# Casting w_out's lower left quarter ahead of the frames' last parts, and issuing the gate's rows behind the first roots

## The chip, the core and the metric

The kernel runs on one core of a Trainium2 chip. The time is the device time of one execution in microseconds (us); lower is better. The engines that matter are TensorE (PE, matrix products), VectorE (DVE), ScalarE (ACT), GpSimd (POOL), and SyncE (SP), which here only issues DMAs. Each engine takes its instructions strictly in the order in which the built program lists them.

## What is computed

One layer of a streaming encoder for 2048 prompt frames and 32 sample frames of width 1024:

```python
hn = rmsnorm(h, g_mix)
proj = hn @ w_in                                   # 1024 x 3072
...                                                # conv mixer and pooling mixer give yA, yB
h = h + jnp.concatenate([yA, yB], axis=-1) @ w_out     # 1024 x 1024
gate = jax.nn.sigmoid(rmsnorm(h, g_ple) @ w_ple_gate)  # 1024 x 1024
h = h + (p @ w_ple) * gate
return rmsnorm(h, g_final)
```

Everything is float32. The kernel reaches that precision on PE by splitting a number into a rounded part (the *cast*, made on ACT) and the *rest* (the number minus its cast, made on DVE), and by forming three products of such parts for each product.

## The kernel before

The program has three stages: the input projection with the mixers (to about 537 us), the w_out stage (to about 706 us), and the embedding products and the gate stage. The change is in the first two pairs of the w_out stage.

**A pair.** The w_out stage takes the mixers' output y from memory (`y_d`, transposed) and goes over the frames in pairs of 128. A pair is multiplied by the 1024 x 1024 weight with seven half-sized products instead of eight (`seven`), each 12 matmuls of 128 x 512. Weights and frames are cut into quarters for it: the weight's quarters 11, 21 (lower left) and 22 (lower right) and the combinations T1 to T4; the frame parts 11, 12, 22 and the combinations S1 to S4. Three banks of PSUM hold the sums and give the tiles their names: `x_o`, `y_o`, `z_o`. The order on PE within a pair is 11·11 (x_o), the first half of S1·T1 (z_o), S2·T2 (x_o), the second half of S1·T1, S3·T3 (x_o), 12·21 (y_o), S4·22 (z_o), and 22·T4 (x_o). Between two products that share a bank, DVE or ACT reads the bank out (`carry` and `out` in `h_ops`, lines 1335 and 1340). So 22·T4 may not start before DVE has added S3·T3 to the tile x.

**Frame parts.** `frame_parts` makes them: a combination is one DVE instruction (`comb`, line 201, tiles `y_fS`), then `split` (lines 80 and 83) makes the cast on ACT and the rest on DVE (tiles `y`, `y_S`). It makes S1, 11, S2 and S3 at once and hands back `more`, which makes 12, S4 and 22. The parts of the next pair are made while PE works on this one; their buffers (pool `cmb`, eight) come free as the products of the pair before end.

**Weight quarters.** The combinations T1 to T4 are made during the last group of the projection. The quarters 11, 21 and 22 are made at the start of the w_out stage by `layout` (casts at line 1408, rests at line 1409; tiles `wo_c` and `wo_d`), from raw rows `wo_q`, which `load_bottom` (line 334) loads. In the first pair, `seven` calls `rest` after its first product: it makes all of 12, S4 and 22 and then, through `tc.issue_after`, the quarters 21 and 22, row block by row block.

**The gate's rows.** The gate's weight has to be scaled row by row with g_ple before the gate stage. That is done on the side in the w_out stage: `scale_gate(k)` loads two halves of a row block (`gs`, line 1387, issued by POOL), and its `rest` scales them on ACT (line 1391) and stores them to `g_d` from ACT's DMA queue (line 1392). `next_gate` first scales what was loaded at the call before, then issues the next loads; it is called at the end of every pair and once inside the second. The two buffers of `gs` are used again and again, so a load waits for the store of the row before. The scaling keeps its place in the program's order on ACT.

**After a pair**, `done_h` squares the finished rows on ACT (line 93), makes the root of the norm on POOL (`rstd_of`, lines 72 and 76) and stores the rows to `h_d` from SP (line 1361).

**What sets the order.** The code calls the steps in one order, and a scheduler arranges them for each engine by estimated costs, within the dependences. `tc.issue_after(ins)` keeps what is called under it behind `ins`, and `tc.keep_in_program_order` keeps an instruction at its place. A tile pool hands a buffer on, and the new user waits for the old ones; `reuse_waits="tile"` sets how finely.

Of the kernel before, what the change touches and what calls it, by code (L numbers as in the profile page):

```python
# [10 lines left out]
F32R = mybir.dt.float32r  # L11
AF = mybir.ActivationFunctionType
ALU = mybir.AluOpType
PSUM = bass.MemoryType.PSUM

P = 128
# [11 lines left out]
NH = D // 2  # L28
KH = KC // 2
# [5 lines left out]
def trunk(ctx, tc, x_p, x_s, c_conv, c_pool, p_p, p_s, g_mix, w_in, conv_w, conv_b, pool_w,  # L35
          pool_scale, w_out, g_ple, w_gate, w_ple, g_fin, y_p, y_s, sc_p, sp_p, sc_s, sp_s):
    nc = tc.nc
# [28 lines left out]
    nhalf = const.tile([P, 1], F32, name="nhalf")  # L66
    nc.gpsimd.memset(nhalf, -0.5)

    def rstd_of(ssq, n, name, r=None):

        ms = sm.tile([P, 1], F32, tag="ms", name=f"ms_{name}")
        nc.gpsimd.tensor_scalar(ms[:n], ssq[:n], scalar1=1.0 / D, scalar2=EPS,  # L72
                                op0=ALU.mult, op1=ALU.add)
        if r is None:
            r = sm.tile([P, 1], F32, tag="rstd", name=f"rstd_{name}")
        nc.gpsimd.tensor_tensor(r[:n], ms[:n], nhalf[:n], op=ALU.pow)  # L76
        return r

    def split(hi, lo, src, eng=nc.vector, later=False):
# [108 lines left out]
    def frame_parts(cmb, tmp, name, a11, a12, a21, a22):  # L188

        A = {}

        def put(q, src):
            A[q] = cmb.tile([P, KH, 2, P], F32R, tag="c", name=f"{name}_{q}")
            return split(A[q][:, :, 0], A[q][:, :, 1], src)

        def comb(q, x, y, op):
            t = tmp.tile([P, KH, P], F32, tag="s", name=f"{name}_f{q}")  # L200
            nc.vector.tensor_tensor(t, x, y, op=op)
            return t

        s1 = comb("S1", a21, a22, ALU.add)
        put("11", a11)
        s2 = comb("S2", s1, a11, ALU.subtract)
        put("S2", s2)
        put("S1", s1)
        put("S3", comb("S3", a11, a21, ALU.subtract))

        def more():
            put("12", a12)
            put("S4", comb("S4", a12, s2, ALU.subtract))
            return put("22", a22)

        return A, more

    def seven(name, A, W, carry, out, between={}, late=False, in_parts=False, first_tile=False, end=None):

        step = lambda c: between[c]() if c in between else None
        frames_late, weights_late = (FINE, FINE[::2] + FINE[1:2]) if in_parts else (None, None)
        X, Y, Z = (bank(f"{c}_{name}") for c in "xyz")

        def lower(*parts):
            for ks in parts:
                product(Z, A["S1"], W["T1"], P, ks.start == 0, ks)
            return carry(Z, (1, 1)) if ks.stop == KH else None

        parts = range(KH // 2), range(KH // 2, KH)
        product(X, A["11"], W["11"], P, True, order=frames_late)
        c1 = carry(X, (0, 0))
        step(1)

        def upper():
            product(Y, A["12"], W["21"], P, True, order=weights_late)
            out(Y, c1, (0, 0))

        if not late:
            upper()
        if late:
            lower(parts[0])
        step(2)
        product(X, A["S2"], W["T2"], P, False)  # L250
        c2 = carry(X, (0, 1))
        step(3)
        c3 = lower(parts[1]) if late else lower(range(KH))
        step(4)

        def right():
            product(Z, A["S4"], W["22"], P, False, order=weights_late)
            out(Z, c2, (0, 1))

        if first_tile:  # L260
            right()
        product(X, A["S3"], W["T3"], P, False)
        out(X, c3, (1, 1))
        step(5)
        if late:
            upper()
        if not first_tile:
            right()
        step(6)
        if end is not None:  # L270
            end(X)
            return
        product(X, A["22"], W["T4"], P, False)
        out(X, None, (1, 0))
# [67 lines left out]
    with ExitStack() as s1:  # L342
        pool = lambda name, bufs: s1.enter_context(tc.tile_pool(name=name, bufs=bufs))
# [16 lines left out]
        def put(piece, src, later=False):  # L360

            split(piece[:, :, 0], piece[:, :, 1], src, later=later)
# [405 lines left out]
        rows = ftile("rows").rearrange("p k n -> p (k n)")[:112, :P]  # L768
# [502 lines left out]
        for gi, tbs in enumerate(GROUPS):  # L1271
            if gi == 2:

                frames_in.close()
                t = slot("hn_4")
# [3 lines left out]
                W = sums_slots("wo")  # L1279
# [35 lines left out]

    with ExitStack() as s2:
        pool = lambda name, bufs: s2.enter_context(tc.tile_pool(name=name, bufs=bufs, reuse_waits="tile"))
        w3, qa, xh, st, ss, cmb = (pool(*a) for a in (
            ("w3", 1), ("qa", 2), ("xh", 3), ("st", 4), ("ss", 3), ("cmb", 8)))

        def quarters(name, W):
            c = halves(slot(f"{name}_c"))
            d = {h: w3.tile([P, KH, NH], F32R, tag=f"d{h}", name=f"{name}_d{h}") for h in (1, 0, 2)}
            W.update({"11": c[:2], "21": (c[2], d[0]), "22": (d[1], d[2])})

        def whole_quarters(W, k, top, bot):
# [6 lines left out]
        def h_ops(x, n, name, bare=False, two=False):  # L1333

            add = lambda o, a, b: nc.vector.tensor_tensor(o, a, b, op=ALU.add)  # L1335

            def carry(ps, at):
                t = st.tile([P, NH], F32, tag="t", name=f"c_{name}_{at[0]}{at[1]}")
                if bare and at != (1, 0):
                    nc.scalar.copy(t[:n], ps[:n])  # L1340
                    return t
                add(t[:n], ps[:n], half_of(x, at, n))
                if two:
                    add(t[:n], ps[n:2 * n], t[:n])
                return t

            def out(ps, c, at):
                t = half_of(x, at, n)
                if bare and at != (1, 0):
                    add(t, t, c[:n])  # L1350
                    c = None
                add(t, ps[:n], t if c is None else c[:n])
                if two:
                    add(t, ps[n:2 * n], t)

            return carry, out
# [22 lines left out]
        def scale_gate(k):  # L1379

            ts = [qa.tile([P, NH], F32, tag="q", name=f"gs_{k}_{half}") for half in range(2)]
            rows = w_gate.rearrange("(q k c) n -> k q c n", q=4, k=KC)[k]
            for half, t in enumerate(ts):
                nc.gpsimd.dma_start(t, rows[:, :, half * NH:half * NH + NH])

            def rest():
                for half, t in enumerate(ts):  # L1390
                    tc.keep_in_program_order(nc.scalar.activation(t, t, AF.Copy, scale=vec[:, 100 + k:101 + k]))
                    nc.scalar.dma_start(g_d[k * P:k * P + P, half * NH:half * NH + NH], t)

            return rest
# [8 lines left out]
        def layout(parts):  # L1403
            for k in range(KH):
                for q, t, c in ("11", tops[k // 2], k % 2), ("21", bots[k], 0), ("22", bots[k], 1):
                    if q in parts:
                        hi, src = W[q][0][:, k], t[:, c * NH:c * NH + NH]
                        nc.scalar.copy(hi, src)
                        hold.append(nc.vector.tensor_tensor(W[q][1][:, k], src, hi.bitcast(F32), op=ALU.subtract))
# [1 line left out]
        quarters("wo", W)  # L1411
        layout(["11"])

        def rest():

            with tc.issue_after(more().ins):
                layout(["21", "22"])

        S = {}
        more = prep_h(0)  # L1420
# [9 lines left out]
        for i in range(0, NT - 1, 2):  # L1430
            with tc.issue_after(loaded[-1].ins):
                x = [load_rows(xh, "x", i + b, x_p) for b in range(2)] if i else [first_x, second_x]
            seven(f"o{i}", S.pop(i), W, *h_ops(x, P, f"o{i}", i == 0), {0: {1: rest}, 2: {3: next_gate}}.get(i, {}), True, i == 0)
            for b in range(2):
                done_h(i + b, x[b])
            last = i + 4 == NT - 1
            if last:
                n = tiles[NT - 1][1]
                A = short("yl", load_y(NT - 1, n), n)
            if i + 2 < NT - 1:  # L1440

                with tc.issue_after(loaded[-1].ins), tc.issue_after(hold[-1].ins):
                    more = prep_h(i + 2)
                more()
            if last:
                x = load_rows(xh, "x", NT - 1, x_p, x_s)
                plain("ol", A, W, n, *h_ops([x], n, "ol", two=True))
                done_h(NT - 1, x)
            next_gate()
# [29 lines left out]
        W = sums_slots("wg")  # L1479
# [245 lines left out]
        S = {}  # L1725
        n = tiles[NT - 1][1]
# [6 lines left out]
        h, e = (load_rows(*a) for a in ((xh, "h", NT - 1, h_d), (ya, "e", NT - 1, e_d)))  # L1733
        plain("gl", A, W, n, *short_ops(h, e, n))
        done_g(NT - 1, h)
        for i in range(0, NT - 3, 2):
            A = S.pop(i)
            h = [load_rows(xh, "h", i + b, h_d) for b in range(2)]
# [35 lines left out]
```

## Time and profile before

| | |
|---|---|
| median of 3 runs | 921.37 us (920.61 to 921.42) |
| the profiled execution | 921.02 us, its span 919.2 us |
| PE busy | 905.7 us (99%) |
| DVE, ACT, POOL busy | 722.4, 481.2, 159.8 us |
| PE on the chain that ended last | 91% |
| mean DMA rate | 223 GB/s |

The span is the time from the first to the last instruction of the program on the core; the execution's own time is 1.8 us longer. In the rows of a timeline stand the start in us, the duration in us, the engine, the source line, the operation, the tile written and the tiles read, and the number of instructions that a row merges; in brackets the engine's idle time before it and what ended that. SPq and ACTq are DMA issues. In the rows of the chain stand start, duration, and what the chain ran through. In the rows of DMA issues stand the number of DMAs, the size of each, and the median time from issue to landing.

### The profile page before, as it was taken

How to read it: one execution, taken by the hardware profiler on the slowest of the kernel's cores; microseconds unless marked ns; L12 is line 12 of the kernel's file. 1: busy time of each engine (PE TensorE's matmuls, PEld its weight loads, DVE VectorE, ACT ScalarE, POOL GpSimd, SP SyncE). 2: the span in 40 equal slices, each digit the busy share in tenths (PEclk: the TensorE clock that was granted, in tenths of full speed). 3: DMA queues.
4: the chain of work that ended last, by engine and by line, in shares of the span. 5: the costliest groups of instructions: out<-in, count | busy, mean ns of one | idle time of the engine just before them, and what ended most of it. 6: DMA issues, size and time to landing. Idle time of an engine off the chain costs nothing.

```text
span 919.2 us, 13202 instructions
## 1 busy us (share of the span) xinstructions
PE 905.7 (99%) x4529; PEld 822.7 (90%) x4529; DVE 722.4 (79%) x1236; ACT 481.2 (52%) x894; POOL 159.8 (17%) x307
## 2 busy tenths in 40 slices
PE   8999999999999999999999999999999999999996
PEld 6999999999999999999999987888878878888885
DVE  6996989999576989795777679665558658889885
ACT  7744565654445555443545356334336755555554
POOL 3111222121000333210000120111203301111113
PEclk9999999999999999999999999999999999999998
DMA  9357687798945898638975469865777984676564
GB/s 262 93 145 217 168 249 230 234 294 287 413 131 168 251 227 225 216 122 296 274 228 173 155 243 291 267 189 177 237 228 231 354 263 143 203 242 235 188 209 169
DMA packets 138447, 205.12 MB, mean 223 GB/s; under 512 B 13116, under 2 KB 101724, under 8 KB 137101
## 3 DMA queue, kind: packets, MB, share of 16 engines
q1 hardware_dynamic: 117773, 139.41, 48.9%
q0 software_dynamic: 17872, 59.45, 19.8%
q10 hardware_dynamic: 2736, 5.44, 1.8%
q8 instruction: 35, 0.57, 0.3%
q14 instruction: 31, 0.25, 0.1%
HBM read 136.60 MB, written 67.64 MB: 222 GB/s over the span
## 4 chain that ended last, share of the span: by engine, by line
PE 91%; DVE 3%; DMA 2%; ACT 2%; issue 1%; POOL 0%; SPq 0%; POOLq 0%; DVEq 0%; ACTq 0%
PE x_g L175 9%; PE x_o L175 9%; PE x_zab L591 7%; PE x_zbv L591 6%; PE x_ch L591 5%; PE z_g L175 5%; PE e L107 4%; PE z_o L175 4%; PE z_zab L591 3%; PE h L591 3%; PE z_zbv L591 3%; PE z_ch L591 3%; PE b L591 3%; PE za L591 3%; PE zb L591 2%; PE c L591 2%
## 5 line engine op out<-in xcount | busy, mean ns | idle before, releaser
L80 ACT CAST y_S<-y_fS 128x512 fp32r<-128x512 f32 x32 | 19.5, 622 | 42.2 <-PE x_o L175 20.4
L175 PE MATMUL x_g<-wg_b,g_S 128*128 128x512 f32 x128 | 35.7, 389 | 0.0
L175 PE MATMUL x_o<-wo_b,y_S 128*128 128x512 f32 x128 | 35.6, 390 | 0.0
L591 PE MATMUL x_zab<-B,w_zab_S 128*128 128x416 f32 x168 | 34.2, 352 | 0.2 <-ACT V L987 0.2
L591 PE MATMUL z_zab<-B,w_zab_S 128*128 128x416 f32 x168 | 34.3, 351 | 0.0
L591 PE MATMUL x_zbv<-B,w_zbv_S 128*128 128x416 f32 x168 | 34.2, 352 | 0.0
L591 PE MATMUL z_ch<-B,w_ch_S 128*128 128x416 f32 x168 | 34.1, 351 | 0.0
L591 PE MATMUL z_zbv<-B,w_zbv_S 128*128 128x416 f32 x168 | 34.0, 351 | 0.0
L591 PE MATMUL x_ch<-B,w_ch_S 128*128 128x416 f32 x168 | 34.0, 351 | 0.0
L107 PE MATMUL e<-wq,pps 128*128 128x512 f32 x144 | 33.1, 390 | 0.0
L591 PEld LDWEIGHTS x_zab<-B,w_zab_S 128*128 128x128 f32 x168 | 31.3, 188 | 0.9 <-ACT V L987 0.5
L107 PEld LDWEIGHTS e<-wq,pps 128*128 128x128 f32 x144 | 27.0, 188 | 5.6
L591 PEld LDWEIGHTS z_zbv<-B,w_zbv_S 128*128 128x128 f32 x168 | 31.4, 188 | 0.3
L591 PEld LDWEIGHTS x_ch<-B,w_ch_S 128*128 128x128 f32 x168 | 31.4, 188 | 0.3
L591 PEld LDWEIGHTS z_ch<-B,w_ch_S 128*128 128x128 f32 x168 | 31.3, 188 | 0.3
L591 PEld LDWEIGHTS z_zab<-B,w_zab_S 128*128 128x128 f32 x168 | 31.3, 188 | 0.3
L591 PEld LDWEIGHTS x_zbv<-B,w_zbv_S 128*128 128x128 f32 x168 | 31.3, 188 | 0.4
L1542 DVE SCALAR_TENSOR_TENSOR h<-h,rstd_f,g_bc 128x1024 f32<-128x1024 f32 (+1 forms) x15 | 19.3, 1284 | 14.0 <-POOL rstd_f L76 14.0
L80 ACT CAST y<-y 128x512 fp32r<-128x512 f32 x24 | 14.8, 618 | 29.4 <-PE z_o L175 12.8
L1335 DVE TENSOR_TENSOR c_o<-x_o,x 128x512 f32<-128x512 f32 x14 | 9.7, 691 | 25.7 <-PE x_o L175 25.7
L72 POOL TENSOR_SCALAR ms_f<-ssq_f 128x1 f32<-128x1 f32 (+1 forms) x15 | 6.6, 441 | 128.8 <-ACT junk L93 128.5
L175 PEld LDWEIGHTS x_o<-wo_b,y_S 128*128 128x128 f32 x128 | 23.9, 188 | 5.2 <-ACT c_o L1340 0.3
(591 smaller groups left out, 2694.9 us busy)
## 6 DMA issues: line engine op xcount, KB each, us to landing
y<-y_d SPq DMA_DIRECT2D x16, 512.0 KB, 6.0
x<-in_x_prompt_dram SPq DMA_DIRECT2D x16, 512.0 KB, 6.0
h_d<-x SPq DMA_DIRECT2D x16, 512.0 KB, 4.3
h<-h_d SPq DMA_DIRECT2D x16, 512.0 KB, 3.5
xt<-in_x_prompt_dram SPq DMA_DIRECT2D x15, 512.0 KB, 7.8
e<-e_d SPq DMA_DIRECT2D x15, 512.0 KB, 5.2
out_dram<-h POOLq DMA_DIRECT2D x14, 512.0 KB, 3.0
p_dT<-T POOLq DMA_DIRECT2D x12, 512.0 KB, 6.0
```

What stands on the lines that cost most here:

```text
L72: nc.gpsimd.tensor_scalar(ms[:n], ssq[:n], scalar1=1.0 / D, scalar2=EPS, op0=ALU.mult, op1=ALU.add)
L80: ins = nc.scalar.copy(hi, src)
L107: nc.tensor.matmul(ps, pps[:, a, k], wp[k][b][:, cs], start=k + q == 0, stop=k == 1 and q == 2)
L175: nc.tensor.matmul(ps[:n], lhs[:, k, a, :n], w[b][:, k], start=start and k + q == 0, stop=k == KH - 1 and q == 2, skip_group_check=True)
L591: nc.tensor.matmul(ps[:, :NB], lhs[:, k, x], b[:, k, y], start=start and k + q == 0, stop=stop and k == KH - 1 and q == 2, skip_group_chec ...
L1335: add = lambda o, a, b: nc.vector.tensor_tensor(o, a, b, op=ALU.add)
L1542: nc.vector.scalar_tensor_tensor(h[:n], h[:n], rf[:n], g_bc[:n], op0=ALU.mult, op1=ALU.mult)
```

## The change

It has three parts.

1. `more` is cut into three calls: `more(0)` makes part 12, `more(1)` makes S4, `more(2)` makes 22. In the first pair the quarter 21 is laid out behind part 12 (called after the first product), and S4, then the quarter 22, and then part 22 are called ahead of S3·T3.
2. The tile `d2` (the rests of quarter 22) moves from pool `w3` to a pool `w2` of its own, which stands behind `qa` in memory; so `qa`, which holds the gate's rows, lies where d2 began.
3. The roots are collected in a list, and the loads of the gate's rows are issued behind the last root made so far: for the first row that is the first pair's second root.

```diff
+    roots = []
...
-        nc.gpsimd.tensor_tensor(r[:n], ms[:n], nhalf[:n], op=ALU.pow)
+        roots.append(nc.gpsimd.tensor_tensor(r[:n], ms[:n], nhalf[:n], op=ALU.pow))
...
-        def more():
-            put("12", a12)
-            put("S4", comb("S4", a12, s2, ALU.subtract))
+        def more(i):
+            if i == 0:
+                return put("12", a12)
+            if i == 1:
+                return put("S4", comb("S4", a12, s2, ALU.subtract))
             return put("22", a22)
...
-        w3, qa, xh, st, ss, cmb = (pool(*a) for a in (
-            ("w3", 1), ("qa", 2), ("xh", 3), ("st", 4), ("ss", 3), ("cmb", 8)))
+        w3, qa, w2, xh, st, ss, cmb = (pool(*a) for a in (
+            ("w3", 1), ("qa", 2), ("w2", 1), ("xh", 3), ("st", 4), ("ss", 3), ("cmb", 8)))
...
-            d = {h: w3.tile([P, KH, NH], F32R, tag=f"d{h}", name=f"{name}_d{h}") for h in (1, 0, 2)}
+            d = {h: (w2 if h == 2 else w3).tile([P, KH, NH], F32R, tag=f"d{h}", name=f"{name}_d{h}") for h in (1, 0, 2)}
...
-            for half, t in enumerate(ts):
-                nc.gpsimd.dma_start(t, rows[:, :, half * NH:half * NH + NH])
+            with tc.issue_after(roots[-1].ins):
+                for half, t in enumerate(ts):
+                    nc.gpsimd.dma_start(t, rows[:, :, half * NH:half * NH + NH])
...
-        def rest():
-            with tc.issue_after(more().ins):
-                layout(["21", "22"])
+        def lower_left():
+            with tc.issue_after(more(0).ins):
+                layout(["21"])
+        def lower_right():
+            with tc.issue_after(more(1).ins):
+                layout(["22"])
+            more(2)
...
-            seven(..., {0: {1: rest}, 2: {3: next_gate}}.get(i, {}), True, i == 0)
+            seven(..., {0: {1: lower_left, 4: lower_right}, 2: {3: next_gate}}.get(i, {}), True, i == 0)
...
-                more()
+                for part in range(3):
+                    more(part)
```

More of the change, by code (lines that the diff above doesn't have):

```diff
@@ L1432, in trunk @@
                 x = [load_rows(xh, "x", i + b, x_p) for b in range(2)] if i else [first_x, second_x]
-            seven(f"o{i}", S.pop(i), W, *h_ops(x, P, f"o{i}", i == 0), {0: {1: rest}, 2: {3: next_gate}}.get(i, {}), True, i == 0)
+            seven(f"o{i}", S.pop(i), W, *h_ops(x, P, f"o{i}", i == 0), {0: {1: lower_left, 4: lower_right}, 2: {3: next_gate}}.get(i, {}), True, i == 0)
             for b in range(2):
```

## The prediction

> **What bounds the kernel now.** I read the page first, then the chain that ended last between 530 and 600 us, then the engines' timelines from 536 to 592 us, then the DMA issues.
>
> ```profile
> span 919.2 us, 13202 instructions
> PE 905.7 (99%) x4529; PEld 822.7 (90%) x4529; DVE 722.4 (79%) x1236; ACT 481.2 (52%) x894; POOL 159.8 (17%) x307
> ```
>
> PE is busy for 99% of the span, so time is saved only where PE stands still, and lost only where something new makes it stand. The change touches the first two pairs of frame tiles of the w_out stage. The chain there:
>
> ```profile
> 545.35 2.79 PE x_o L170 x12
> ...
> 553.67 0.07 ACT y L80
> 553.74 0.46 issue
> 554.20 0.62 ACT wo_c L1408
> ...
> 557.42 0.53 ACT wo_c L1408
> 557.95 0.04 issue
> 557.99 2.35 PE y_o L170 x9
> ...
> 563.06 5.44 PE x_o L175 x24
> ...
> 582.10 5.44 PE x_o L175 x24
> ```
>
> The first pair runs from 545.35 to 565.78 (the last product of a pair and the first of the next share one row of 24, half of 5.44 each): 20.43 us. The second runs from 565.78 to 584.82: 19.04. The first pair is 1.39 us too long, and the chain says where: it leaves PE at 553.6 and goes through the eight weight casts of ScalarE (ACT) until 557.99. That is the one stall that this change can remove, and **1.39 us is the most it can be worth**.
>
> **Part 1: the lower left quarter earlier.** On ACT:
>
> ```profile
> 548.66 0.62 ACT L80 CAST y<-y 128x512 fp32r<-128x512 f32 x1
> 552.30 0.62 ACT L80 CAST y_S<-y_fS 128x512 fp32r<-128x512 f32 x1 [3.02 <-PE x_o L175]
> ...
> 554.20 0.62 ACT L1408 CAST wo_c<-wo_q 128x512 fp32r<-128x512 f32 x1
> 554.72 0.62 ACT L1408 CAST wo_d<-wo_q 128x512 fp32r<-128x512 f32 x1
> ...
> 557.33 0.61 ACT L1408 CAST wo_c<-wo_q 128x512 fp32r<-128x512 f32 x1
> ```
>
> ACT casts frame part 12 at 548.66, then stands 3.02 us for the buffer of S4, and only afterwards casts the weights, at a pitch of 0.52 (554.20 to 554.72), lower left (wo_c) and lower right (wo_d) in turn. In the changed program's order the four wo_c casts follow part 12 directly: 549.2 to 551.4, inside the 3.02 us of idle. VectorE (DVE) makes their rests behind its own part 12:
>
> ```profile
> 549.60 0.68 DVE L83 TENSOR_TENSOR y<-y,y 128x512 fp32r<-128x512 f32 x1
> 552.96 0.69 DVE L83 TENSOR_TENSOR y_S<-y_fS,y_S 128x512 fp32r<-128x512 f32 x1 [2.67 <-ACT y_S L80]
> ```
>
> 550.2 to 552.7 in its own idle 2.67 us. The y_o product wants its first wo_c at 556.3 and its first rest eight matmuls later, 558.1; both are ready over 3 us ahead. The rows must have landed:
>
> ```profile
> wo_q<-in_w_out_dram SPq DMA_DIRECT2D x4, 512.0 KB, 5.5
> 539.59 2.28 SPq L334 DMA_DIRECT2D wo_q<-in_w_out_dram  x4
> ```
>
> Issued from 539.59 to 541.87 and 5.5 us on the way give 545 to 547.5; if the last is 3 us later behind the others, it is still there for its cast at 550.8. What is late next: the four wo_d casts (after the copy of x_o and S4, 553.4 to 556.1), their rests on DVE (554.2 to 557.2), part 22 (ACT 556.0, DVE 557.2). The z_o product wants them from 559.0, 22·T4 at 561.8. Nothing waits. I take **1.3 us off** (between 0, if a hand-off takes it, and 1.39); PE then starts the second pair at 564.5, and its 22·T4 at 582.10 - 1.3 = 580.8.
>
> The d2 tile in a pool of its own only changes which older buffers are waited for; the rests of wo_d now wait for two ACT-issued stores of the embedding instead of one of them and POOL's. Costed at nothing.
>
> One load moves with part 22:
>
> ```profile
> 551.18 4.25 SPq L326 DMA_DIRECT2D y<-y_d  x2
> ```
>
> The second of these, half of the third pair's frames, waits on SP for DVE's rest of part 22 and goes out at 555.05; with that rest at 557.2 to 557.9 it goes out 2.8 us later. Nothing else stands in SP's queue until 562, and DVE's first use of it comes at 565.4 or later, 7.5 us on; within part 2's relief of the queues I cost it at nothing, at worst 1 us, which the wait of part 2 swallows too.
>
> **Part 2: the gate's loads behind the roots.** What is removed: two loads of 256 KB that now start at 548.
>
> ```profile
> 548.08 1.43 POOL L1387 DMA_DIRECT2D gs<-in_w_ple_gate_dram  x2 [0.91 <-DMA e_d<-eout]
> gs<-in_w_ple_gate_dram POOLq DMA_DIRECT2D x2, 256.0 KB, 11.5
> y<-y_d SPq DMA_DIRECT2D x1, 512.0 KB, 14.2
> 553.00:563.00 10.00, 9.44 (x40) 7.04 (x39) 9.92 (x17) 6.30 (x12) 0.00 (x0) 1.00 1.11 266
> ```
>
> The last row is a window of 10 us: behind the five engines' busy time stand the clock, the share of the DMA engines, 1.11, and 266 GB/s. The gate's loads shared these full queues with the frames (one load of them took 14.2 us). The second pair's frames are on the way, and in the new order DVE wants them at 558.4. Half a MB at 266 GB/s is 1.9 us, so the frames come up to that much sooner than DVE's first use at 561.58. If they do not, DVE runs up to 3 us late and the second pair's first copy-out of x_o, which the new order puts behind two sums and two rests of the frames, is late by up to 2.7 us. I take 0 to 1 us, which the next wait swallows.
>
> What is added is a wait. Both loads now stand on POOL behind the second root of the pair, and ACT takes their scaling in program order:
>
> ```profile
> 568.45 0.55 POOL L76 TENSOR_TENSOR rs_h<-ms_h,nhalf 128x1 f32<-128x1 f32 x1
> 569.45 0.72 ACT L1391 ACTIVATE gs<-gs,vec 128x512 f32<-128x512 f32 x1
> 570.59 0.72 ACT L1391 ACTIVATE gs<-gs,vec 128x512 f32<-128x512 f32 x1
> 572.86 0.61 ACT L80 CAST y_S<-y_fS 128x512 fp32r<-128x512 f32 x1
> 574.59 1.29 DVE L83 TENSOR_TENSOR y_S<-y_fS,y_S 128x512 fp32r<-128x512 f32 x2
> 576.99 0.69 DVE L1335 TENSOR_TENSOR x<-x_o,c_o 128x512 f32<-128x512 f32 x1
> ```
>
> The root ends at 569.0 now, so at 567.8 then, and the loads go out at 567.8 and 568.5. ACT reaches the first scaling at about 568.3 and stands until the data are there. Queued behind it on ACT are the casts of S1 and S3 for the third pair; behind those, on DVE, their rests, two sums, and then the add of x_o (line 1335) that frees PE's bank for 22·T4. From the landing of the second load to that bank: scaling 0.62, cast 0.66, then on DVE from the first rest to the end of the add 576.99 + 0.69 - 574.59 = 3.1, and 0.17 of hand-overs: **4.55 us**. PE wants the bank at 580.8, so a landing after 576.25 costs PE one for one.
>
> When does it land? Rows of single loads:
>
> ```profile
> gs<-in_w_ple_gate_dram POOLq DMA_DIRECT2D x1, 256.0 KB, 7.3
> gs<-in_w_ple_gate_dram POOLq DMA_DIRECT2D x1, 256.0 KB, 5.3
> gs<-in_w_ple_gate_dram POOLq DMA_DIRECT2D x1, 256.0 KB, 9.3
> gs<-in_w_ple_gate_dram POOLq DMA_DIRECT2D x16, 256.0 KB, 8.1
> ```
>
> 7.3 is the load issued at 574.91, 5.3 the one at 579.45 in emptied queues, 9.3 the one at 606.88. Two back to back are shown once, at 548: about 11.5 each, and the second goes out 0.7 later, so some 12 to 12.6 from the first issue. From below: 7.3 and 1.3 for the second, 8.6. At 568 four or five 512 KB transfers (a store of h, frames and x) stand in SP's queue, as at 606.88; so I take 9.3 + 1.7 = 11, landing 578.8. The bank is free at 583.35 and PE stands **2.55 us**. Ends: 576.4 (0.15 us) and 580.4 (4.15 us).
>
> [...]
>
> POOL's own roots stand behind the second row's loads from here on; they are read in the gate stage, from 750 us, so that is free. Those loads wait for the first row's store, land near 588 to 590 and hold ACT ahead of the third pair's casts in the same way; PE's need there is 2.55 us later as well, so I count nothing, and up to 1.3 us at the upper end.
>
> **The sum.** Minus 1.3, plus 2.55: +1.25 us on the profiled execution (span 919.2, its own time 921.02): 922.3. The median of the three runs is 0.35 above that execution, so 921.37 + 1.25 = **922.6 us**. The later pairs and the gate stage keep their order of PE work, so the shift is carried to the end. 0.2%, 1.84 us, is about what a measurement of this kernel can tell from no change; the forecast lies within it.
>
> **Rivals.** [...] 0.18.
>
> *The wait for the gate's rows outgrows the gain* (slower by over 0.2%): the landing after 579.4, 11.6 us from the first issue, gives a stall of 3.15 and more, +1.85 and more. For it: the only back to back pair took over 12. Typical 580.2, +2.65: 924.0; with the second row's wait up to 925.2. 0.37.
>
> *The first part does not do what it says*: the casts come early but DVE or a weight row is late, the 1.39 stays, the new wait comes on top, and little is gained anywhere. PE then wants the bank at 582.1, so the same landing costs 1.25: 922.6 too, from 921.4 to 924.4. 0.05.
>
> **How the numbers follow.** The forecast (landing 576.4 to 579.4, 920.2 to 923.2) has 0.40. Slower by over 0.2%: the second rival and a little of the last, 0.39. Faster by over 0.2% needs more than the whole 1.39 us, so something not seen here: 0.05. Within: 0.56. The range leaves out little of the first rival and the tail of the second: 920.0 to 925.0.
>
> **What would show it.** Right: in the profile after, no wait of y_o for wo_c, the wo_c casts near 549 to 551.4, the second pair's start on PE near 564.5; gate loads on POOL right behind a root near 568; ACT idle ahead of the scaling (L1397 there) for 6 to 10 us, released by the gate's load; and a PE gap ahead of 22·T4 of the second pair, released by DVE's add. Wrong: no such gap (then 920.1), a gap of over 4 us, or PE waiting elsewhere, for the copy-out of x_o near 569.

## The result and the profile after

The changed kernel takes 926.59 us (median of seven runs) against 921.42 for the kernel before beside it: the ratio is 1.0054, with a 95% interval from 1.0042 to 1.0066. It is slower by 5 us. (One of the seven executions, at 942.84 us, was in a slower state of the chip, with a mean clock of 0.919, and is left out of the ratio.) The forecast was 922.6, in a range up to 925.0, so it was too low, and the time lies outside the range. The profiled execution took 926.59 us with a span of 924.7, 5.5 us more than the span before.

The page of the changed kernel, its head, the shares of the engines and the row of PE's clock:

```profile
span 924.7 us, 13204 instructions
...
PE 908.8 (98%) x4529; PEld 825.1 (89%) x4529; DVE 721.9 (78%) x1236; ACT 481.0 (52%) x894; POOL 159.7 (17%) x307
...
PEclk9999999999999999999999999899999999999999
```

Two things are new. PE is busy for 3.1 us *more* although it computes the same, and one slice of the clock's row is an 8. Then PE's timeline in the two pairs that the change touches (start, length, and in brackets the idle time ahead and what ended it):

```profile
555.91 1.98 PE L172 MATMUL y_o<-wo_c,y 128*128 128x512 f32 x8
...
564.07 2.88 PE L177 MATMUL x_o<-wo_c,y 128*128 128x512 f32 x12
...
577.95 2.88 PE L177 MATMUL z_o<-wo_d,y_S 128*128 128x512 f32 x12
584.50 5.46 PE L177 MATMUL x_o<-wo_T,y 128*128 128x512 f32 x12 [3.67 <-ACT y L82]
```

The first pair's y_o no longer waits, and the second pair starts at 564.07 instead of 565.62. (In this profile the first pair also starts 0.22 sooner, at 544.96.) Ahead of 22\*T4 of the second pair PE stands 3.67 us, and then twelve products take 5.46 us, where the rows above show 2.88 for twelve. Windows say why (busy time of PE, PEld, DVE, ACT, POOL, then the clock, 1.00 being full speed, the share of the DMA engines, and GB/s):

```profile
580.00:584.00 4.00, 0.83 (x4) 0.37 (x2) 2.74 (x5) 2.63 (x6) 1.36 (x2) 0.97 0.28 85
584.00:590.00 6.00, 5.50 (x13) 4.37 (x14) 4.65 (x8) 2.87 (x5) 0.50 (x2) 0.50 0.44 161
590.00:592.00 2.00, 2.00 (x9) 1.56 (x9) 0.69 (x1) 1.19 (x3) 0.24 (x1) 0.86 0.92 247
```

From 583.7 to 590.5, for 6.83 us, PE was granted half its clock: 13 products in a window where 26 fit. Products start 0.427 us apart there, against 0.227. Now POOL, ACT and DVE, the engines that PE was waiting for:

```profile
567.92 1.51 POOL L1393 DMA_DIRECT2D gs<-in_w_ple_gate_dram  x2
577.18 0.72 ACT L1397 ACTIVATE gs<-gs,vec 128x512 f32<-128x512 f32 x1 [8.78 <-DMA gs<-in_w_ple_gate_dram]
579.49 0.72 ACT L1397 ACTIVATE gs<-gs,vec 128x512 f32<-128x512 f32 x1 [1.59 <-DMA gs<-in_w_ple_gate_dram]
580.61 1.14 ACT L82 CAST y_S<-y_fS 128x512 fp32r<-128x512 f32 x2 [0.40 <-ACT gs L1397]
581.26 1.29 DVE L85 TENSOR_TENSOR y_S<-y_fS,y_S 128x512 fp32r<-128x512 f32 x2 [8.03 <-ACT y_S L82]
...
583.68 0.68 DVE L1339 TENSOR_TENSOR x<-x_o,c_o 128x512 f32<-128x512 f32 x1
```

That is the chain of the prediction, link by link: loads behind the root, ScalarE (ACT) standing 8.78 and 1.59 us for them, the casts of S1 and S3 behind that, then VectorE (DVE), which stood 8.03 us for the first of these casts, then the add that frees the bank at 584.37. (The bracket of 22\*T4 names a cast of ACT instead, since that cast ended last, 0.02 us after the add.)

**The sum of the change.** I measure a pair from its first x_o<-wo_c product to the next pair's. The pairs took 20.44, 19.04 and 19.04 us before, and 19.11, 25.69 and 19.46 now. That is -1.33 for the first, +6.65 and +0.42 for the others, together +5.74; less 0.22 of the earlier start, 5.52. The 7.07 us of loss are 0.28 of hand-overs (short delays of PE at the copies-out of x_o), 3.83 of stand (start of 22\*T4's first product against 0.227 us behind the last z_o product), and 2.96 of half clock (24 products in 8.40 us instead of 5.44).

### The profile page after: what moved, and what is told of

It is laid out like the page before. It is cut to its first block, busy times and chain, and to the rows that moved or that the text cites. A ratio compares the mean times of both kernels' runs of the same rounds, so it can differ in the third digit from the quotient of the medians.

```text
span 924.7 us, 13204 instructions
## 1 busy us (share of the span) xinstructions
PE 908.8 (98%) x4529; PEld 825.1 (89%) x4529; DVE 721.9 (78%) x1236; ACT 481.0 (52%) x894; POOL 159.7 (17%) x307
## 3 DMA queue, kind: packets, MB, share of 16 engines
q10 hardware_dynamic: 2736, 5.44, 1.8%
## 4 chain that ended last, share of the span: by engine, by line
PE 77%; DVE 6%; DMA 3%; issue 1%; ACT 1%; POOL 1%; POOLq 0%; ACTq 0%; DVEq 0%
PE x_g L177 9%; PE x_o L177 8%; PE x_zab L595 6%; PE z_g L177 5%; PE x_zbv L595 5%; PE e L109 4%; PE x_ch L595 4%; PE z_o L177 4%; PE z_zab L595 3%; PE z_ch L595 2%; PE z_zbv L595 2%; PE y_g L177 2%; PE za L595 2%; PE b L595 2%; PE v L595 2%; PE c L595 2%
## 5 line engine op out<-in xcount | busy, mean ns | idle before, releaser
L177 PE MATMUL x_o<-wo_T,y 128*128 128x512 f32 x96 | 25.6, 420 | 3.7 <-ACT y L82 3.7
```

The costliest lines, as they stand in the source:

```text
L177: nc.tensor.matmul(ps[:n], lhs[:, k, a, :n], w[b][:, k], start=start and k + q == 0, stop=k == KH - 1 and q == 2, skip_group_check=True)
```

## The experiments

As in the prediction, the first part is the early casts and the second the gate's loads behind the roots; the tile d2 has its new place in every run but e2. Each kernel was timed beside the kernel before on one chip. The pair lengths come from the profiles, as above; pairs not named took 19.04 us, or a few tenths more now and then. The last column is the median against that of the kernel before, with the ratio's interval.

| run | 1st pair | 2nd | 3rd | elsewhere | against before |
|---|---|---|---|---|---|
| before | 20.44 | 19.04 | 19.04 | | |
| changed | 19.11 | 25.69 | 19.46 | | +5.2, 1.0042 to 1.0066 |
| e1 early gate loads | 19.11 | 22.47 | 19.04 | | +0.6, 1.000 to 1.002 |
| e2 roots alone | 20.44 | 22.10 | 19.38 | | +4.2, 1.0020 to 1.0059 |
| e3 hold | 19.11 | 23.69 | 19.04 | | +2.3, 1.0011 to 1.0034 |
| e4 first root | 19.11 | 27.62 | 19.04 | | +6.9, 1.0055 to 1.0085 |
| e5 16 products | 19.11 | 23.11 | 20.13 | | +4.4, 1.0033 to 1.0061 |
| e6 8 products | 19.12 | 23.13 | 20.21 | | +4.3, 1.0036 to 1.0070 |
| e7 call in 5th pair | 19.11 | 19.37 | 19.04 | 5th 21.03, 6th 20.64 | +2.3, 1.0006 to 1.0032 |
| e8 changed, again | 19.12 | 25.03 | 19.06 | | +4.3, 1.0033 to 1.0069 |
| e9 call in last pair | 19.12 | 19.37 | 19.04 | 11.4 ahead of the gate | +9.9, 1.0095 to 1.0125 |
| e10 call behind all | 19.11 | 19.35 | 19.04 | 10.7 ahead of the gate | +8.9, 1.0084 to 1.0112 |
| e11 call in 7th pair | 19.11 | 19.39 | 19.04 | 7th 23.91 | +6.0, 1.0046 to 1.0092 |
| e12 mark | 19.12 | 19.35 | 19.04 | | -1.0, 0.9978 to 1.0001 |

What lies ahead of w_out moves from run to run (the first pair began between 543.9 and 546.9 us, at 545.2 in the kernel before), so the pair lengths tell more than one median.

**e1: the first part without the second.**

```diff
-            with tc.issue_after(roots[-1].ins):
-                for half, t in enumerate(ts):
-                    nc.gpsimd.dma_start(t, rows[:, :, half * NH:half * NH + NH])
+            for half, t in enumerate(ts):
+                nc.gpsimd.dma_start(t, rows[:, :, half * NH:half * NH + NH])
```

> The changed kernel without its second part: the lower left quarter is cast early, the gate's rows are loaded as early as in the kernel before (near 548). Theory A (the loss is ScalarE standing for the late gate loads, the tensor engine standing behind that, and then running at half clock): no stand of PE ahead of 22*T4 of the second pair, clock 1.00 throughout, the 1.33 us of the first part stay: 920.1 us, 919.5 to 921. Theory B (the early casts themselves, by their order on VectorE and ScalarE, make the second pair late): the stand of 3.7 us stays, 926 to 927. Theory C (the early loads crowd the second pair's frames, which the new order needs sooner): the copy-out of x_o of the second pair is late by up to 2.7 us, 921.5 to 923, and the second pair's frames land near 559.5 and 561.3 as before instead of 555.6 and 557.1.

Theory C held in place and about in size, but not by the frames that I named. The 1.33 us are there, no half clock, no stand ahead of 22\*T4; but the second pair's x_o waits for its copy-out (POOL, DVE and PE):

```profile
552.71 1.43 POOL L1392 DMA_DIRECT2D gs<-in_w_ple_gate_dram  x2 [6.71 <-PE z_o L177]
567.68 0.69 DVE L203 TENSOR_TENSOR y_fS<-y,y 128x512 f32<-128x512 f32 x1 [3.04 <-DMA y<-y_d]
570.96 0.50 PE L177 MATMUL x_o<-wo_a,y_S 128*128 128x512 f32 x1 [2.92 <-DVE c_o L1339]
```

The gate's loads did not go out near 548, as I had expected: they wait for a z_o product of PE (the bracket of the first row), probably because d2's move gave their buffers another place in memory. So they fall between the third pair's two loads. The second pair's frames had landed by 556.0. Late are the *third* pair's: their second load goes out at 556.6, behind the gate's two loads, and lands at 567.6; in the changed kernel it goes out at 557.6 and lands at 562.6. DVE, in program order, sums these frames ahead of the copy-out. So the second part of the change was not idle: it clears the queues for this load. Without it the first part gives its gain back.

**e2: the second part alone**, the issue behind the newest root put into the kernel before.

> The kernel before with the second part of the change alone: the casts stay where they were, each row of the gate is loaded behind the newest root. Theory A: the first pair keeps its 1.39 us of stall (y_o waits for wo_c), the loads go out near 569.3, land near 580.5, the bank is free near 585.4 and PE wants it at 582.1: a stand of 3.3 us, alone 924.7; with a drop to half clock behind it, about 3 us more, 927.7. Theory B (the early casts are at fault): 921.4, no stand.

ACT's and PE's timelines:

```profile
576.69 0.72 ACT L1394 ACTIVATE gs<-gs,vec 128x512 f32<-128x512 f32 x1 [5.93 <-DMA gs<-in_w_ple_gate_dram]
580.16 0.72 ACT L1394 ACTIVATE gs<-gs,vec 128x512 f32<-128x512 f32 x1 [2.74 <-DMA gs<-in_w_ple_gate_dram]
582.86 3.00 PE L177 MATMUL z_o<-wo_d,y_S 128*128 128x512 f32 x12 [2.76 <-DVE c_o L1337]
```

The wait for wo_c is back, and ACT stands for the gate's loads as in the changed kernel. PE's stand comes at another place, S4\*22 instead of 22\*T4, since VectorE's order differs in this program; 2.76 us against the 3.3 expected. In this profile the clock stayed at 1.00. With neither the early casts nor d2's move in it, the kernel loses 4.2 us, so the loss comes from the gate's loads, and theory B (the early casts) falls.

**e3: the first row behind the last rest of quarter 22.**

```diff
-            with tc.issue_after(roots[-1].ins):
+            with tc.issue_after((roots[-1] if k else hold[-1]).ins):
```

> The changed kernel with the first row of the gate behind the last rest of the lower right quarter (near 557) instead of the second root (567). Theory A: the loads land 566 to 569, ScalarE stands for them 2 us at most and well ahead of PE's need at 580.7; no stand of PE, no half clock, the first part's 1.33 us stay: 920.1 us, 919.5 to 921. If the loads at 557 collide with frames: up to 922. Theory B (the early casts are at fault): 926 to 927.

The edge did not hold the first row. That rest is an instruction of DVE and the loads stand on POOL, which is probably why; the loads went out at 555.48, as soon as PE had released their buffer, and the last rest of the quarter ended at 558.8. The run is therefore much like e1, with the same wait of x_o for its copy-out (2.74 us, third pair's frames at 570.3). It is worth its row for the clock: a stand of 2.74 us brought half clock for 3.41 us here, where 2.92 us in e1 did not. Two windows, in the stand and behind it:

```profile
571.00:574.00 3.00, 0.34 (x2) 0.30 (x2) 2.97 (x6) 0.65 (x2) 0.00 (x0) 1.00 0.66 250
575.20:578.50 3.30, 3.30 (x9) 2.61 (x8) 0.74 (x2) 0.54 (x1) 1.44 (x2) 0.50 1.06 358
```

**e4: the first row behind the pair's first root** (`roots[-1 if k else -2]`).

> The changed kernel with the first row of the gate behind the first root of the pair (ends near 565.1) instead of the second (567.9): the loads go out 2.8 us sooner, land near 576.6, and PE stands about 1.0 us (0.3 to 2) ahead of 22*T4 instead of 3.7. Theory A (half clock is the consequence of the long stand): a stand of 1 us doesn't bring it; clock 1.00, 921.1 us, 920.4 to 922.2. Theory D (the products behind the stand are slow for another reason, their operands or the transfers beside them): the 24 products take 8.4 us instead of 5.44 here too, 923.8, 923 to 925.

A miss of both theories, 929.3 us. The loads did go out sooner, at 566.36. But with that the scheduler put the first scaling on ACT *ahead of* a cast of the third pair that stands before it in the changed kernel. This cast's rest stands on DVE ahead of a copy-out that PE wants some eight us sooner than the bank of 22\*T4 (ACT, DVE and PE):

```profile
575.44 0.72 ACT L1397 ACTIVATE gs<-gs,vec 128x512 f32<-128x512 f32 x1 [6.82 <-DMA gs<-in_w_ple_gate_dram]
576.70 0.69 DVE L85 TENSOR_TENSOR y<-y,y 128x512 fp32r<-128x512 f32 x1 [6.67 <-ACT y L82]
579.87 5.33 PE L177 MATMUL x_o<-wo_b,y_S 128*128 128x512 f32 x12 [5.86 <-DVE c_o L1339]
```

PE stands 5.86 us, and from 578.04, inside the stand, it has half clock for 6.83 us. What a load's landing costs depends on what was queued behind its reader.

**e5 and e6: products in place of the stand.**

```diff
+        def filler():
+            ps = tbank("filler")
+            for q in range(16):
+                nc.tensor.matmul(ps, W["22"][0][:, 0, :P], W["22"][0][:, q % KH], start=q == 0, stop=q == 15, skip_group_check=True)
...
-            ... 2: {3: next_gate}}.get(i, {}), True, i == 0)
+            ... 2: {3: next_gate, 6: filler}}.get(i, {}), True, i == 0)
```

e6 has 8 of these products, about 1.8 us of work at 0.227 us each, so about half of the stand stays.

> The changed kernel with 16 products of the same form put on PE right ahead of 22*T4 of the second pair (their result is used by nothing): 16 x 0.227 = 3.6 us of work where PE stood for 3.67 us. The bank comes free as before. Theory A (half clock follows from PE standing): the stand falls to 0.3 us or less, the clock stays 1.00, the 24 products behind it take 5.44 us instead of 8.4; 2.9 us less than the changed kernel on this chip (about 923.6 if that one is at 926.6), 2.3 to 3.3 less. Theory D (those products are slow for their operands or the transfers beside them): no difference, within 0.5.

> [...]

PE's timeline and a window of e5, then both of e6:

```profile
581.26 3.79 PE L1438 MATMUL filler<-wo_d 128*128 128x512 f32 x16
584.89 3.00 PE L177 MATMUL x_o<-wo_T,y 128*128 128x512 f32 x12
...
592.77 0.50 PE L177 MATMUL x_o<-wo_a,y_S 128*128 128x512 f32 x1 [0.80 <-DVE c_o L1339]
```

```profile
585.00:591.00 6.00, 6.00 (x28) 4.94 (x28) 4.63 (x8) 2.73 (x5) 0.75 (x2) 1.00 0.49 171
```

```profile
586.17 2.97 PE L177 MATMUL x_o<-wo_T,y 128*128 128x512 f32 x12 [1.76 <-ACT y L82]
```

```profile
586.20:592.00 5.80, 5.80 (x26) 4.82 (x27) 4.72 (x8) 2.49 (x4) 0.74 (x2) 1.00 0.47 167
```

The same products with the same operands and the same transfers beside them run at full clock (1.00 in both windows) when PE does not stand ahead of them, and also when it stands 1.76 us. Theory D falls: half clock follows from the stand, 3.67 us in the changed kernel. The mean clock over the span, which is on record for every run, agrees: 0.996 to 0.999 in the nine runs of e5, 0.993 to 0.997 in the nine of e8. The second pair is 2.6 us shorter than in the changed kernel (1.9 shorter than in e8). But the time of the whole was not: 926.70 and 926.60 against 926.51 for e8. About 1.1 us of it was lost again in the third pair, whose x_o waits 0.80 us for a copy-out that these programs have in another place of VectorE's order. And an execution of e5 or e6 takes 2.2 to 2.5 us beyond its span, where one of e8 takes 1.8; why is open. The expected 2.9 us did not show in the median; the mechanism shows in the profiles.

**e8: the changed kernel again, beside e5 to e7.**

> The changed kernel again, beside the three others on this chip: 5.0 us over the kernel before (4 to 6). [...]

PE's timeline (line numbers are one higher in this file), then windows:

```profile
585.34 4.54 PE L178 MATMUL x_o<-wo_T,y 128*128 128x512 f32 x12 [3.89 <-ACT y L83]
```

```profile
585.30:588.60 3.30, 3.26 (x8) 2.61 (x9) 3.27 (x6) 0.72 (x1) 0.00 (x0) 0.50 0.34 121
588.70:592.00 3.30, 3.30 (x15) 2.68 (x15) 1.51 (x3) 3.00 (x6) 0.78 (x3) 1.00 0.68 223
```

Same place, same wait, but in this execution the half clock lasts 3.41 us and costs 1.7 us, not 3.0.

**e7, e9, e10 and e11: the extra call elsewhere.** The change has nine calls of `next_gate` for eight rows; the one in the second pair makes a row's loads and its scaling lie only half a pair apart. These runs move that call: `2: {3: next_gate}` becomes `8:` (e7), `14:` (e9), `12:` (e11), or the call stands behind `embedding_chunks("wq")` (e10). The first row is then scaled at the end of the second pair, behind all of the third pair's casts.

> The changed kernel with the extra scaling call moved from the second pair to the fifth (frame tiles 8 and 9): the first row is loaded behind the roots as in the changed kernel, but scaled only at the end of the second pair, behind all of the third pair's casts on ScalarE. Theory A: ScalarE doesn't stand between 568 and 580, the bank ahead of 22*T4 is in time, no half clock there, and the 1.33 us of the first part stay: 1.3 us under the kernel before, 0.8 to 1.6, unless the fifth pair's call stands in the same way (its loads, near 625, took 5.5 us for the second row in the changed kernel, against 9.2 and 10.8 here, so a stand of at most 1 us there). Theory B (the early casts make the late bank): the stand ahead of 22*T4 stays, 5 us over the kernel before.

> As the run with the call in the fifth pair, with the extra call in the last pair of frame tiles (14 and 15), which has no further pair's casts behind it on ScalarE. Theory A: the pairs of w_out take 19.11 us for the first, at most 19.4 for the second and 19.04 for the others; nothing stands there; 1.0 to 1.3 us under the kernel before, if the gate's last rows, scaled later among the casts of the gate's weights, still come in time for the gate stage (56.2 us from the last pair's tail to the gate's first product). If they don't, up to 3 us are lost there.

> As before it, with the extra call behind the last of all pairs (behind the embedding's weights): the pairs as in that run, 19.11, at most 19.4, 19.04; the last row of the gate is loaded and scaled latest here. 1.0 to 1.3 us under the kernel before by theory A; up to 3 us lost where the gate's weights wait for that row.

> As those, with the extra call in the pair ahead of the last (12 and 13), with the last pair's casts behind it on ScalarE. Theory A: the second pair as in those (at most 19.4), and a stand in this pair or the next as the fifth pair had it (2.0 and 1.6 us there): the loss is not a matter of the second pair, but of loads and scaling half a pair apart; 0 to 2.5 us over the kernel before. If the stand in the second pair had come from its crowded queues alone, nothing stands here: 1.0 to 1.3 us under it.

In all four the second pair takes 19.35 to 19.39 us: the stand is gone, with the early casts and the late loads of the first row unchanged. That shows the cause: ACT standing in program order ahead of the third pair's casts. In all four the price was paid where the call went. ACT and PE in e11, then POOL and PE in e10:

```profile
672.04 0.72 ACT L1397 ACTIVATE gs<-gs,vec 128x512 f32<-128x512 f32 x1 [10.02 <-DMA gs<-in_w_ple_gate_dram]
675.30 4.59 PE L177 MATMUL z_o<-wo_d,y_S 128*128 128x512 f32 x12 [2.95 <-DVE c_o L1339]
```

```profile
717.87 1.43 POOL L1393 DMA_DIRECT2D gs<-in_w_ple_gate_dram  x2 [1.26 <-DMA g_d<-gs]
722.28 8.18 PE L109 MATMUL e<-wq,pps 128*128 128x512 f32 x24 [4.92 <-DMA pps<-pp_d]
```

In e11 a stand of 2.95 us comes back in the seventh pair, with half clock for 3.41 us behind it: 23.91 us. In e7 the fifth and sixth pair pay 3.6 us, in waits of 0.8, 0.7 and 1.3 us and what lies around them. In e9 and e10 the last row stands on POOL ahead of loads that the embedding wants; PE waits 3.45 and 5.46 us there in e9 and 4.92 in e10, has half clock for 6.83 us in each, and some 11 us are lost, which I had put at 3 at most. The e11 profile was the fastest of its runs by 2.2 us, so its +6.0 is more than its pairs show.

**e12: loads between the third pair's frames and the roots.** A small operation on POOL that reads the first pair's result out of x_o, and the first row behind it.

```diff
-            with tc.issue_after(roots[-1].ins):
+            with tc.issue_after((roots[-1] if k else mark[-1]).ins):
...
+        def marker():
+            m = sm.tile([P, 1], F32, tag="ms", name="mark")
+            mark.append(nc.gpsimd.tensor_scalar(m, x[1][:, NH:NH + 1], scalar1=1.0, scalar2=0.0, op0=ALU.mult, op1=ALU.add))
...
-            ... {0: {1: lower_left, 4: lower_right}, 2: ...
+            ... {0: {1: lower_left, 4: lower_right, 5: marker}, 2: ...
```

> The changed kernel with the first row of the gate behind a small operation on POOL that reads the first pair's x_o result (out at about 558.2), so that its loads go out near 558.7 and 559.4: behind the issue of the third pair's second load of frames (557.6), 9 us ahead of where the changed kernel issues them. Theory A: the frames of the third pair land by 565.5, where VectorE wants them, the gate's loads by 569.5 or so; ScalarE, on which the first scaling now stands ahead of the third pair's casts, stands 1 to 3 us, and PE's next need for VectorE behind that, the copy-out of x_o ahead of S3*T3 near 572.6, is met or missed by up to 1 us; no half clock. First pair 19.11, second 19.1 to 20.1 us; 0.3 to 1.3 us under the kernel before. If the frames are as late as in the run with the loads in front of them (567.6), the second pair takes about 22 and the kernel is 1 to 2 us over.

POOL's and ACT's timelines, and one window over both pairs:

```profile
558.51 1.15 POOL L1425 TENSOR_SCALAR mark<-x 128x1 f32<-128x1 f32 x1 [11.31 <-DVE x L1339]
559.61 1.46 POOL L1393 DMA_DIRECT2D gs<-in_w_ple_gate_dram  x2
567.52 0.72 ACT L1397 ACTIVATE gs<-gs,vec 128x512 f32<-128x512 f32 x1
568.65 0.72 ACT L1397 ACTIVATE gs<-gs,vec 128x512 f32<-128x512 f32 x1
```

```profile
545.00:585.00 40.00, 40.00 (x176) 32.62 (x175) 34.84 (x56) 22.38 (x42) 7.19 (x11) 1.00 0.91 301
```

The profile shows no moment of these 40 us in which PE stands. The third pair's second load is issued at 557.8, ahead of the gate's, and lands at 562.9; the gate's rows land at 565.4 and 567.7, and ACT takes them without idling. The first part's gain stays, 1.32 us, less 0.31 of hand-overs in the second pair. The ratio is 0.9990, from 0.9978 to 1.0001: about 1 us less than the kernel before, at the edge of what can be told from none, and, by the last column of the table, 5 to 6 us less than the changed kernel.

## Why the prediction was wrong

**Part 1, right.** From ACT's timeline of the changed kernel:

```profile
548.95 2.18 ACT L1414 CAST wo_c<-wo_q 128x512 fp32r<-128x512 f32 x4
```

The casts stand where ACT idled (549.2 to 551.4 was forecast), y_o did not wait, the first pair became 1.33 us shorter (forecast 1.3) in every kernel with the early casts. (The chain before ran through seven of the eight weight casts, up to the last wo_c, not all eight; nothing hangs on it.) The move of one load was costed at nothing "within part 2's relief of the queues": right with that relief; e1 shows 2.92 us without it, more than the 1 us I had set as the worst.

**Part 2, the wait itself: the mechanism and the place right, the size too small.** Every sign that I had named for being right is there. The loads went out at 567.92 (567.8 forecast), the first landed at 577.1, the second at 579.46 (578.8), and from the landing to the bank's release by DVE's add at 584.37 it took 4.91 us (4.55). PE wanted the bank at 580.67 (580.8). So the stand was 3.83 us where I said 2.55: 0.66 from the landing, 0.36 from the chain behind it, the rest from PE's start and the hand-over to PE. That is inside the ends 0.15 and 4.15 that I gave for it, and the rival by which the wait outgrows the gain, a landing after 579.4, was the case that came. The second row's wait cost nothing, as forecast: its loads landed at 587.4 and 588.6, and PE does not stand in the third pair.

**The step that failed** is "a landing after 576.25 costs PE one for one". It cost 3.83 us of stand and 2.96 us more, since the clock fell to 0.50 behind it. The same error stands in the first paragraph, by which time is lost "only where something new makes it stand": this stand had a price behind it as well. With -1.33 and +0.28 of hand-overs that is +5.74 on the pairs; by that rival's own sum, -1.3 + 3.83, the time would have been 923.9, inside the range. I had read that PE is busy for 99% of the span and had no row of a stand longer than 0.53 us in the w_out stage to price a longer one by. The trace of before does hold a sign, at its end: the clock falls to 0.50 at 913.86, 2.02 us after PE's last product.

## What to carry to other kernels

Price a stand of PE twice: by its own length, and by what the clock may do behind it. The shortest stand with half clock behind it was 2.74 us here (e3), and 3.45 us in e9 had none; in the changed kernel 3.83 us of stand cost 2.96 us more. Before a load is issued later, look at what is queued behind its reader, on that engine and on the next ones, and find the latest issue that all of them can bear; here the good place lay behind the frames' load at 557.8 and well ahead of 566 (e12, e4). An edit that looks like two parts may be one: the early casts kept their gain only where the gate's loads came behind the third pair's frames (e1, e12), and neither part was faster than the kernel before without the other.

## What the runs showed of the hardware

PE's granted clock fell to 0.50 behind some stands and stayed at 1.00 behind others. With the stands' lengths as the timelines give them in brackets, it fell with 2.74 us (e3), 2.95 (e11), 3.67 (changed kernel), 3.89 (e8), 4.92 (e10), 5.46 (e9) and 5.86 (e4), and stayed with 1.76 (e6), 2.76 (e2), 2.92 (e1) and 3.45 (e9). So between 2.74 and 3.45 us the length alone does not tell the two apart here, and what else decides was not shown. Half clock lasted 3.41 us in e3, e8 and e11, and 6.83 us in the changed kernel, e4, e9 and e10; the changed kernel and e8 are the same program, and why it lasted twice as long in one was not shown.

That the drop comes in some executions of a kernel and not in others is an estimate from the spread of e2 (924.1 to 928.6) and e3 (922.1 to 926.4) over their runs, since only one execution of each was profiled. But the mean clock is on record for all: in e3 it is 0.995 or 0.996 in four runs of 925.1 to 926.4 us, and 0.997 or more in the other eight, with a median of 923.9.

Loads of 256 KB from POOL's queue took between 5.2 us (e8, 582.31 to 587.54) and 12.6 us (e1, second load, 553.44 to 566.04). In the first stretch the DMA engines' share was 0.38 at 108 GB/s, in the second 1.12 at 273 GB/s.
